# Rotary of the queries in a hybrid trunk: the product with the sines moved ahead of the exchange

## The chip, the cores and the metric

The kernel runs on one core of one Trainium2 chip. A core has five engines, each with its own instruction queue that is executed in order: TensorE (PE; its weight loads are listed as PEld), VectorE (DVE), ScalarE (ACT), GpSimd (POOL) and SyncE (SP), which here only issues DMAs. TensorE writes its results into eight PSUM banks of 128 x 512 fp32 values; DVE and ACT read them there, and everything else lives in SBUF. The metric is the device time of one execution in microseconds (us); the time of a kernel is the median of its runs.

## The reference, cut to what matters

A trunk of two layers over 1024 tokens of width 1024. The even layer has a sparse attention; its 8 attention heads and 8 indexer heads, each of 64 channels, get rotary positions:

```python
def apply_rope(x, cos, sin):
    x1, x2 = jnp.split(x, 2, axis=-1)
    return jnp.concatenate([x1 * cos - x2 * sin, x1 * sin + x2 * cos], axis=-1)
...
    q = apply_rope(q.reshape(B, L, A_HEADS, A_HEAD_DIM), cos[:, None], sin[:, None])
    k = apply_rope(c_kv @ w_uk, cos, sin)
    qi = apply_rope(qi.reshape(B, L, IDX_HEADS, IDX_DIM), cos_i[:, None], sin_i[:, None])
    ki = apply_rope(ki, cos_i, sin_i)
```

The indexer's scores (rectified products of qi and ki, weighted and summed over the heads) choose 256 keys per query, over which q attends. Beside the attention the layer has a pooling mixer over four groups of channels; then come an output projection and an MLP. The odd layer is a gated delta rule and an MLP. All of it is fp32.

## The kernel before, in words

**Layout.** Activations are kept transposed: channels on the 128 partitions, 512 tokens (half of the sequence) on the free axis. The two halves are called s = 0 and s = 1. A matrix product of fp32 precision is made of three (`mm3`, lines 245 to 247): every operand is held as a high part (a rounded copy by ACT, line 165) and a low part (the remainder, a subtraction, line 169, by POOL or DVE). Weights come in chunks by SP (line 200, into `raw`), are copied by ACT and get their remainder from POOL, into the rings `w` and `wm`.

**Even layer.** `even_steps` walks over a list of projections: the latent and the indexer's key first, then four pairs of indexer heads ("qi"), four groups of the pooling mixer ("u"), and four pairs of attention heads ("q"). For each it makes the projection, eight groups of three matmuls into one PSUM bank of the tag "g" (there are two of these), and starts a generator that picks the bank up; then it makes one step of every earlier generator (`step_late`). So what stands behind a `yield` is issued one projection later or more. The pooling group reads its bank with DVE (line 573).

**Rotary of a query pair.** One bank holds two heads, 64 partitions each. For the exchange of the two halves of a head, partitions are exchanged in blocks of 32: partition p gets what lies at p ^ 32. `swapped` (line 502) copies the bank to SBUF with ACT (tile "at") and exchanges the blocks of that copy by four DMAs on SP (line 508), 64 KB each, into a second "at". A step later `query_stacks` (line 350) calls `rotate` (line 334): POOL multiplies the copy by the cosines (line 339, into "temps"), DVE the exchanged parts by the sines (line 340, into "temps") and adds the two (line 341). The table of the sines carries the sign already: -1 on the first 32 partitions of each head, +1 on the others. Then ACT copies the high parts of the two heads, and POOL (s = 0) or DVE (s = 1) makes the remainders (lines 359 and 360). Keys are rotated by the same `rotate` from two banks, the second of which TensorE has filled with the exchanged product, all on DVE.

**Buffers.** `Ring` hands out rotating buffers. "temps" (`self.T`) has five, used by the rotary, the pooling mixer, the sums of squares and the normalized inputs of the MLP (line 327). "at" (`self.A`) has four, used by the rotary, the latent, the indexer's key and the transposed probabilities of the attention (lines 746 to 756). The sines and cosines of one half of the sequence lie in one "rope" buffer, which the other half's overwrite (line 462).

**Order.** The generators set the order in which instructions are issued to a planner, which has its own estimates of durations and puts each engine's instructions into a queue by priority and by when it thinks that their inputs and buffers are ready. The selection of keys (`topk`, lines 671 to 686), a long chain of small DVE and ACT operations, is interleaved with the projections, and for s = 1 the scores (lines 371, 542 to 547) and the attention of s = 0 (`attend`). The last four query projections (s = 1) run beside the normalization for an early part of the MLP, whose matmuls fill the rest of the stage. On the chip the queues are then executed in this fixed order.

Of the kernel before, what the change touches and what calls it, by code (L numbers as in the profile page):

```python
# [18 lines left out]
OP = mybir.AluOpType  # L19
# [105 lines left out]
class Trunk:  # L125
# [205 lines left out]
        return x  # L331


    def rotate(self, p, ps2, s, p_in_psum=False):

        nc = self.nc
        cos, sin = self.ropes[s][:, 0:512], self.ropes[s][:, 512:1024]
        t1, r = self.T.get(), self.T.get()
        (nc.vector if p_in_psum else nc.gpsimd).tensor_tensor(t1, p, cos, op=OP.mult)
        nc.vector.tensor_tensor(r, ps2, sin, op=OP.mult)  # L340
        nc.vector.tensor_tensor(r, r, t1, op=OP.add)
        return r
# [7 lines left out]
    def query_stacks(self, p, s, ring):  # L350

        nc = self.nc
        r = self.rotate(*p, s)
        q = ring.parts()
        a, b = q[:, 0:512], q[:, 512:1024]
        self.copy(a[0:64], r[0:64])
        self.copy(b[64:128], r[64:128])
        eng = nc.vector if s else nc.gpsimd
        eng.tensor_tensor(a[64:128], r[0:64], a[0:64].bitcast(F32), op=OP.subtract)
        eng.tensor_tensor(b[0:64], r[64:128], b[64:128].bitcast(F32), op=OP.subtract)  # L360
        return q
# [92 lines left out]
    def even_latent(self, s, ps):  # L454

        nc = self.nc
        sq, cf = self.T.get(), self.A.get()
        nc.vector.tensor_tensor(cf, ps, self.rb, op=OP.mult)
        nc.scalar.activation(sq, cf, AF.Square)
        yield  # L460
        rope = self.RO.get()
        nc.sync.dma_start(rope, self.I["rope"][s])
        self.ropes.append(rope)
        y = self.rstd_cols(sq, P)
        yield
        r = self.over_partitions(y)
        nc.vector.scalar_tensor_tensor(cf, cf, self.prm[:, R_KVN:R_KVN + 1], r, op0=OP.mult, op1=OP.mult)
        yield
        p1, p2 = self.bank(), self.bank()
        nc.tensor.matmul(p1, self.wkv[:, 0:128], cf, start=True, stop=True)  # L470
        nc.tensor.matmul(p2, self.wkv[:, 128:256], cf, start=True, stop=True)
        self.kst.append(self.key_stacks(self.rotate(p1, p2, s, True), self.KS))
        pv = self.bank()
        for j in range(4):
            nc.tensor.matmul(pv[:, j * 64:(j + 1) * 64], cf[:, j * P:(j + 1) * P], self.wkv[:, 256:320],
                             start=True, stop=True)
        va = self.VA.get()
        self.copy(va, pv[:, :256])
        self.vau.append(va)

    def even_index_keys(self, s, ps):

        nc = self.nc
        kw = self.A.get()
        nc.vector.tensor_tensor(kw[:72], ps[:72], self.rb[:72], op=OP.mult)
        yield
        p1, p2 = self.bank(), self.bank()
        for ps, w in ((p1, self.ident), (p2, self.c(C_SWAP))):
            for at in (0, 64):
                nc.tensor.matmul(ps[at:at + 64], w[:64, 0:64], kw[:64], start=True, stop=True)  # L490
        self.kis.append(self.key_stacks(self.rotate(p1, p2, s, True), self.KI))
        pw = self.bank()
        for j in range(4):
            nc.tensor.matmul(pw[:, j * 8:(j + 1) * 8], kw[:72, j * P:(j + 1) * P],
                             self.cx[:72, C_WSEL:C_WSEL + 8], start=True, stop=True)
        wi = self.small(32, "wi")
        b4 = lambda t: t.rearrange("p (b h) -> p b h", b=4)
        nc.vector.scalar_tensor_tensor(b4(wi), b4(pw[:, :32]), float(np.float32(8 ** -0.5)) / 8,
                                       self.scales[s][0][:, :, None].to_broadcast([P, 4, 8]), op0=OP.mult, op1=OP.mult)
        self.wis.append(wi)  # L500

    def swapped(self, ps):

        pc = self.A.get()
        self.copy(pc, ps)
        ps2 = self.A.get()
        for at in range(0, P, 32):
            self.nc.sync.dma_start(ps2[at:at + 32], pc[at ^ 32:(at ^ 32) + 32])
        return pc, ps2

    def even_index(self, s, p, ps):

        pc = self.swapped(ps)
        yield
        self.qis.append(self.query_stacks(pc, s, self.Y))
        if s == 0:
            for _ in range(1 + (p < 3)):
                yield
            for _ in self.index_scores(s, p):
                pass  # L520
# [35 lines left out]

    def even_query(self, s, p, ps):

        pc = self.swapped(ps)
        yield  # L560
        self.qs[s].append(self.query_stacks(pc, s, self.Q))

# [668 lines left out]
    def even(self):  # L1231

        nc, I = self.nc, self.I
        take = lambda g, n=1: [next(g, None) for _ in range(n)]
        with ExitStack() as st:
            ep = self.pool("even", stack=st, side="left")
            self.mask = {i: ep.tile([P, (i + 1) * P], BF16, name=f"mask{i}") for i in range(2, KT)}
            self.KS, self.VA = Ring(ep, "keys", 2, 1024), Ring(ep, "values", 2, 256)
            self.Q, self.A = Ring(ep, "q", 4, 1024), Ring(ep, "at", 4, 512)
            self.PB, self.rb = Ring(ep, "probs", 4, 1024), ep.tile([P, 512], F32, name="rb")  # L1240
            self.room("a", self.W, self.WM, self.W, self.WM, self.W)
            self.kst, self.vau, self.kis, self.ropes = [], [], [], []
# [251 lines left out]
```

## Time and profile before

| | us |
|---|---|
| time, median of 3 runs | 2784.98 (2773.43 to 2786.07) |
| the profiled execution's own time | 2783.84 |
| its span, first to last instruction | 2782.1 |
| PE busy | 2653.8 (95%) |
| DVE busy | 1660.1 (60%) |
| POOL busy | 1227.5 (44%) |
| ACT busy | 1185.8 (43%) |

How to read what follows. A row of a group or of the list of instructions names the line of the kernel, the engine, the operation, the tile written, "<-" and the tiles read (buffer numbers left out: "at", "temps", "ps_g" for a bank of tag g), and the shapes. In the list of instructions the first two numbers are the start and the duration in us, and a bracket gives how long the engine stood idle before and what ended it. In a list of groups, busy us and mean ns of one stand behind the bar, then the idle time before. In the list of waits, the numbers are us in total, how many times, and the longest. "SPq" and the like are the sequencers that issue DMAs. A matmul's end is modelled by the profiler.

### The profile page before, as it was taken

What the parts mean: (1) busy time and instruction counts of PE and PEld (TensorE: products, weight loads), DVE (VectorE), ACT (ScalarE), POOL (GpSimd) and SP (SyncE); (2) the same over time, 40 slices, a digit from 0 to 9 for tenths busy, and PEclk for the clock granted to TensorE, in tenths of its full rate; (3) what the DMA queues carried; (4) which work ended last, traced back from release to release, by engine and by line L of the source; (5) the groups of instructions that cost most, each with busy time, mean ns of one, the idle gap of its engine ahead of it and who ended that gap; (6) DMA issues with size and microseconds to landing.
All of it is one profiled execution on the core that took longest, in us unless ns stands there. A gap on an engine that the chain in (4) does not pass through costs nothing. (4 is left out here: it accounts for less than half of the span.)

```text
span 2782.1 us, 44603 instructions
## 1 busy us (share of the span) xinstructions
PE 2653.8 (95%) x16640; PEld 2094.9 (75%) x16640; DVE 1660.1 (60%) x3587; ACT 1185.8 (43%) x2480; POOL 1227.5 (44%) x1062
## 2 busy tenths in 40 slices
PE   8789989999999999999999999999999999899998
PEld 6566768787777787777777767777777777688886
DVE  5788998734435655655565777655556645633334
ACT  4557767334444543433333344433334333433332
POOL 4653354542245444434454444434444434544442
PEclk9999989999999999999999999999999999999999
DMA  5221223331123222222222212122222222333332
GB/s 192 76 75 35 68 81 98 91 91 54 42 76 96 80 84 73 80 77 78 68 88 73 62 47 64 59 65 77 75 71 73 69 69 87 118 98 95 96 98 76
DMA packets 121068, 220.91 MB, mean 79 GB/s; under 512 B 14098, under 2 KB 15250, under 8 KB 120850
## 3 DMA queue, kind: packets, MB, share of 16 engines
q1 hardware_dynamic: 120850, 218.05, 25.4%
q8 instruction: 131, 2.15, 0.3%
q14 instruction: 87, 0.71, 0.1%
HBM read 209.61 MB, written 4.19 MB: 77 GB/s over the span
## 5 line engine op out<-in xcount | busy, mean ns | idle before, releaser
L169 POOL TENSOR_TENSOR wm<-raw,wm 128x512 fp32r<-128x512 f32 x425 | 562.0, 1323 | 853.9 <-ACT wm L165 840.3
L165 ACT ACTIVATE wm<-raw 128x512 fp32r<-128x512 f32 x425 | 267.3, 629 | 606.2 <-PE ps_g L246 270.7
L169 POOL TENSOR_TENSOR w<-raw,w 128x512 fp32r<-128x512 f32 x222 | 296.7, 1337 | 351.3 <-ACT w L165 330.8
L841 DVE TENSOR_TENSOR h<-ps_d,h 128x512 f32<-128x512 f32 x392 | 267.1, 685 | 134.4 <-PE ps_d L247 132.4
L245 PE MATMUL ps_g<-x,w 128*128 128x512 f32 x644 | 259.5, 403 | 12.1 <-ACT w L165 9.1
L827 DVE SCALAR_TENSOR_TENSOR ps_g<-ps_g,temps 128x512 f32<-128x512 f32 x128 | 89.1, 696 | 291.0 <-ACT temps L825 291.0
L246 PE MATMUL ps_g<-x,w 128*128 128x512 f32 x644 | 257.1, 399 | 4.3 <-DVE x L380 4.1
L247 PE MATMUL ps_g<-x,w 128*128 128x512 f32 x644 | 256.6, 398 | 1.0 <-POOL w L169 1.0
L245 PE MATMUL ps_d<-y,wm 128*128 128x512 f32 x596 | 243.7, 409 | 10.3 <-DVE h L841 8.7
L165 ACT ACTIVATE w<-raw 128x512 fp32r<-128x512 f32 x222 | 139.0, 627 | 258.3 <-PE ps_g L246 180.9
L247 PE MATMUL ps_d<-y,wm 128*128 128x512 f32 x596 | 236.5, 397 | 0.3 <-POOL wm L169 0.2
L246 PE MATMUL ps_d<-y,wm 128*128 128x512 f32 x596 | 236.0, 396 | 0.0
L245 PE MATMUL ps_g<-xb,wm 128*128 128x512 f32 x512 | 207.7, 406 | 5.6 <-ACT qkvz L947 5.0
L247 PE MATMUL ps_g<-xb,wm 128*128 128x512 f32 x512 | 206.4, 403 | 5.5 <-POOL wm L169 5.4
L246 PE MATMUL ps_g<-xb,wm 128*128 128x512 f32 x512 | 205.7, 402 | 0.0
L949 DVE SCALAR_TENSOR_TENSOR qkvz<-temps,conv,qkvz 128x512 f32<-128x512 f32 x144 | 130.8, 909 | 97.9 <-ACT qkvz L947 96.8
L245 PEld LDWEIGHTS ps_g<-x,w 128*128 128x128 f32 x644 | 123.2, 191 | 40.6 <-ACT w L165 9.9
L245 PE MATMUL ps_g<-x,wm 128*128 128x512 f32 x352 | 141.5, 402 | 7.7 <-ACT wm L165 2.9
L246 PEld LDWEIGHTS ps_g<-x,w 128*128 128x128 f32 x644 | 123.0, 191 | 33.3 <-DVE x L380 6.6
L245 PEld LDWEIGHTS ps_d<-y,wm 128*128 128x128 f32 x596 | 112.0, 188 | 44.9 <-DVE h L841 16.9
L246 PE MATMUL ps_g<-x,wm 128*128 128x512 f32 x352 | 140.9, 400 | 4.4 <-DVE x L169 4.4
L247 PE MATMUL ps_g<-x,wm 128*128 128x512 f32 x352 | 141.1, 401 | 3.2 <-POOL wm L169 3.2
(445 smaller groups left out, 6089.5 us busy)
## 6 DMA issues: line engine op xcount, KB each, us to landing
raw<-in_w_dram SPq DMA_DIRECT2D x456, 256.0 KB, 2.7
raw<-in_woi_dram SPq DMA_DIRECT2D x128, 256.0 KB, 2.6
raw<-in_w2q_dram SPq DMA_DIRECT2D x56, 256.0 KB, 2.6
raw<-in_wei_dram SPq DMA_DIRECT2D x52, 256.0 KB, 2.7
raw<-in_weo_dram SPq DMA_DIRECT2D x32, 256.0 KB, 2.7
raw<-in_woo_dram SPq DMA_DIRECT2D x32, 256.0 KB, 2.7
h<-in_xt_dram SPq DMA_DIRECT2D x16, 256.0 KB, 3.0
at<-at SPq DMA_DIRECT2D x64, 64.0 KB, 2.0
```

The source lines that it names most:

```text
L165: self.nc.scalar.activation(out, in_, AF.Copy)
L169: eng.tensor_tensor(lo, full, hi.bitcast(F32), op=OP.subtract)
L245: mm(ps, wh, xh, start=start, stop=False)
L246: mm(ps, wh, xl, start=False, stop=False)
L247: mm(ps, wl, xh, start=False, stop=stop)
L827: nc.vector.scalar_tensor_tensor(ps, ps, 0.0, r, op0=OP.max, op1=OP.mult)
L841: nc.vector.tensor_tensor(h, ps, h, op=OP.add)
L949: nc.vector.scalar_tensor_tensor(acc, pin[:, j:j + 512], cw(j), acc, op0=OP.mult, op1=OP.add)
```

## The change

The product with the sines is taken before the exchange, directly out of the PSUM bank by DVE (`pm`), instead of after it from the exchanged copy. Since the table's sign is then that of the partition from which the value comes, the exchanged product is subtracted instead of added. ACT still copies the bank to SBUF, and POOL multiplies that copy in place by the cosines, now right behind the copy and not one step later. The four DMAs exchange the blocks of `pm` into `m`. What is left for the later step is one subtraction in place on DVE. A query so uses three "at" buffers (`pc`, `pm`, `m`), of which `pc` is held until its high and low parts are made, and no "temps"; the ring "at" grows from four buffers to six. `rotate` is left to the keys alone.

```diff
-    def rotate(self, p, ps2, s, p_in_psum=False):
+    def rotate(self, p, ps2, s):
 
         nc = self.nc
         cos, sin = self.ropes[s][:, 0:512], self.ropes[s][:, 512:1024]
         t1, r = self.T.get(), self.T.get()
-        (nc.vector if p_in_psum else nc.gpsimd).tensor_tensor(t1, p, cos, op=OP.mult)
+        nc.vector.tensor_tensor(t1, p, cos, op=OP.mult)
         nc.vector.tensor_tensor(r, ps2, sin, op=OP.mult)
         nc.vector.tensor_tensor(r, r, t1, op=OP.add)
         return r
...
     def query_stacks(self, p, s, ring):
 
         nc = self.nc
-        r = self.rotate(*p, s)
+        r, m = p
+        nc.vector.tensor_tensor(r, r, m, op=OP.subtract)
         q = ring.parts()
...
-    def swapped(self, ps):
-
-        pc = self.A.get()
+    def rotated(self, ps, s):
+        nc = self.nc
+        cos, sin = self.ropes[s][:, 0:512], self.ropes[s][:, 512:1024]
+        pc, pm = self.A.get(), self.A.get()
+        nc.vector.tensor_tensor(pm, ps, sin, op=OP.mult)
         self.copy(pc, ps)
-        ps2 = self.A.get()
+        nc.gpsimd.tensor_tensor(pc, pc, cos, op=OP.mult)
+        m = self.A.get()
         for at in range(0, P, 32):
-            self.nc.sync.dma_start(ps2[at:at + 32], pc[at ^ 32:(at ^ 32) + 32])
-        return pc, ps2
+            nc.sync.dma_start(m[at:at + 32], pm[at ^ 32:(at ^ 32) + 32])
+        return pc, m
...
     def even_index(self, s, p, ps):
 
-        pc = self.swapped(ps)
+        pc = self.rotated(ps, s)
         yield
...
     def even_query(self, s, p, ps):
 
-        pc = self.swapped(ps)
+        pc = self.rotated(ps, s)
         yield
...
-            self.Q, self.A = Ring(ep, "q", 4, 1024), Ring(ep, "at", 4, 512)
+            self.Q, self.A = Ring(ep, "q", 4, 1024), Ring(ep, "at", 6, 512)
```

More of the change, by code (lines that the diff above doesn't have):

```diff
@@ L471, in even_latent @@
         nc.tensor.matmul(p2, self.wkv[:, 128:256], cf, start=True, stop=True)
-        self.kst.append(self.key_stacks(self.rotate(p1, p2, s, True), self.KS))
+        self.kst.append(self.key_stacks(self.rotate(p1, p2, s), self.KS))
         pv = self.bank()
@@ L490, in even_index_keys @@
                 nc.tensor.matmul(ps[at:at + 64], w[:64, 0:64], kw[:64], start=True, stop=True)
-        self.kis.append(self.key_stacks(self.rotate(p1, p2, s, True), self.KI))
+        self.kis.append(self.key_stacks(self.rotate(p1, p2, s), self.KI))
         pw = self.bank()
```

## The prediction

> **What bounds the kernel now.** The page comes first, then the busy time by stage.
>
> ```profile
> span 2782.1 us, 44603 instructions
> PE 2653.8 (95%) x16640; PEld 2094.9 (75%) x16640; DVE 1660.1 (60%) x3587; ACT 1185.8 (43%) x2480; POOL 1227.5 (44%) x1062
> ...
> 28.00:410.00 382.00, 332.61 (x1478) 246.00 (x1477) 314.75 (x750) 232.69 (x483) 184.82 (x140) 0.92 0.25 77
> 28.00:160.00 132.00, 110.19 (x441) 79.96 (x439) 95.25 (x241) 70.09 (x148) 80.66 (x65) 0.91 0.33 103
> 350.00:410.00 60.00, 47.11 (x174) 35.38 (x173) 56.55 (x89) 36.13 (x65) 33.85 (x23) 0.83 0.27 80
> 410.00:800.00 390.00, 384.25 (x2044) 311.64 (x2043) 222.44 (x485) 188.09 (x336) 149.29 (x112) 0.99 0.24 74
> L340 DVE TENSOR_TENSOR temps<-at,rope x16: 677/690/1785, 51.4 to 397.0; 128x512 f32<-128x512 f32 x16
> ```
>
> The last row is the answer on the tile "at" (least, median, most ns; first and last start). The columns of the stages are PE, PEld, DVE, ACT, POOL, clock, DMA share, GB/s. PE works 95% of the span. After 410 us it is the bound (384.25 of 390). The 16 products of the queries with the sines start between 51.4 and 397.0 us, so the rotary lies in the stage from 28 to 410 us, and there PE idles 382 - 332.61 = 49.4 us while DVE is busy 314.75 of 382 (82%), and 56.55 of 60 at the end. So what the change can win or lose is settled in 49.4 us of PE's idle time, 21.8 of it before 160 us and 12.9 after 350. The whole is 1.8% of the time.
>
> Who holds PE up there, and who holds DVE and SP up, by the list of waits from 25 or 30 to 410 us:
>
> ```profile
> PE ps_t L371 <- DVE h L547: 6.2, 3, 3.4
> PE ps_g L247 <- POOL wm L169: 3.2, 3, 2.0
> PE ps_g L245 <- ACT at L165: 1.6, 1, 1.6
> PE ps_g L245 <- DVE at L458: 1.6, 1, 1.6
> DVE temps L340 <- DMA at<-at: 9.1, 2, 7.8
> SPq L508 <- ACT at L165: 10.9, 4, 4.5
> ```
>
> PE's longest wait of all is for DVE's score sums (L547), not for the rotary's own instructions. DVE stood 9.1 us, in two places, before the product with the sines (L340), since the exchanged parts had not landed.
>
> **The change part by part.** The groups from 28 to 410 us, by form:
>
> ```profile
> L341 DVE TENSOR_TENSOR temps<-temps 128x512 f32<-128x512 f32 x20 | 19.8, 992 | 0.4
> L340 DVE TENSOR_TENSOR temps<-at,rope 128x512 f32<-128x512 f32 x16 | 16.7, 1046 | 9.2 <-DMA at<-at 9.1
> L340 DVE TENSOR_TENSOR temps<-ps_t,rope 128x512 f32<-128x512 f32 x4 | 2.8, 690 | 1.2 <-PE ps_t L490 1.0 <-PE ps_t L471 0.2
> L339 POOL TENSOR_TENSOR temps<-at,rope 128x512 f32<-128x512 f32 x16 | 24.3, 1522 | 5.9 <-ACT at L165 2.1 <-DVE x L169 2.0 <-DVE ps_s L685 0.8
> ```
>
> Removed: 16 products with the sines from SBUF, 1046 ns each, 16.7 us of DVE. Added: 16 products from the bank. The keys already do this one, at 690 ns: 11.0 us. DVE's load falls by 5.7 us. The subtraction replaces the addition (L341) operand for operand, both in SBUF: 992 ns as before. ACT's copy out of the bank stays. The four DMAs of a query stay, on the same SP queue; they now wait for DVE's product instead of ACT's copy.
>
> Why the SBUF form is dearer shows here:
>
> ```profile
> 49.88 2.52 POOL L339 TENSOR_TENSOR temps<-at,rope 128x512 f32<-128x512 f32 x2
> 49.90 0.69 DVE L339 TENSOR_TENSOR temps<-ps_t,rope 128x512 f32<-128x512 f32 x1 [3.38 <-PE ps_t L470]
> 51.37 1.58 DVE L340 TENSOR_TENSOR temps<-at,rope 128x512 f32<-128x512 f32 x1
> ```
>
> While POOL worked from 49.88 to 52.40, DVE's product out of a bank took 0.69 us and the one with two SBUF inputs 1.58. I therefore take 690 for all 16, in whatever company; the other end is 1046, a saving of nothing.
>
> [...]
>
> *Where the 5.7 us lie on the path.* Two places can be followed.
>
> ```profile
> 57.50 0.58 ACT L165 ACTIVATE at<-ps_g 128x512 f32<-128x512 f32 x1
> 60.74 2.43 SPq L508 DMA_DIRECT2D at<-at  x4
> 66.48 1.72 DVE L340 TENSOR_TENSOR temps<-at,rope 128x512 f32<-128x512 f32 x1 [7.85 <-DMA at<-at]
> ...
> 383.40 1.78 DVE L340 TENSOR_TENSOR temps<-at,rope 128x512 f32<-128x512 f32 x1
> 386.81 1.76 DVE L341 TENSOR_TENSOR temps<-temps 128x512 f32<-128x512 f32 x1
> 388.60 1.28 ACT L165 ACTIVATE q<-temps 64x512 fp32r<-64x512 f32 x2 [3.91 <-DVE temps L341]
> 389.90 0.63 ACT L165 ACTIVATE wm<-raw 128x512 fp32r<-128x512 f32 x1
> 390.59 0.57 PE L245 MATMUL ps_g<-x,wm 128*128 128x512 f32 x1 [2.92 <-ACT wm L165]
> ```
>
> At 57.50 a query leaves its bank; SP issues its DMAs only at 60.74, DVE waits until 66.48, and the score work behind it starts late, which PE feels at L547. The new product fits before 60.74, where DVE was idle (from 66.48 - 7.85 = 58.63), so the DMAs are no earlier and DVE still waits; but behind the landing one operation stands instead of two. That is 1.72 us less; I count -1.5, between 0 and the 6.2 that PE lost to L547.
>
> At 383.40 the same operation precedes the addition, ACT's copies and, queued behind them on ACT, a weight for which PE waits 2.92 us. Without it all move up: -1.8, between 0 and -2.9.
>
> The other queries free 0.36 us each on a DVE that is 82% busy while PE idles 13%: some 4 us; I count -1.0, between 0 and -4.
>
> *The buffers.* A query held two "temps" buffers of five (T) and two "at" of four (A); now it holds none of T and three of six of A. From 365 to 387 us the early MLP's normalized inputs pass through T:
>
> ```profile
> 375.70 0.51 PE L245 MATMUL ps_g<-x,wm 128*128 128x512 f32 x1 [2.35 <-ACT x L165]
> 379.79 0.79 PE L246 MATMUL ps_g<-x,wm 128*128 128x512 f32 x1 [3.58 <-DVE x L169]
> ...
> 381.20 1.73 POOL L339 TENSOR_TENSOR temps<-at,rope 128x512 f32<-128x512 f32 x1 [2.01 <-DVE x L169]
> ```
>
> POOL's product of a query waited for a buffer of T that the normalization gave back (L169), so both compete for it. PE lost 2.35 + 3.58 = 5.9 us to these inputs. Freed buffers are worth 0 to -5.9; I take -1.5, near the lower end, as DVE itself is full there. Against it, the products of two queries move from behind this normalization into it: 2 x 0.69 = +1.4.
>
> *The hold of the bank.* There are two banks for projections. A bank was free after ACT's copy; now it needs ACT's copy and DVE's product.
>
> ```profile
> 77.26 0.39 PE L247 MATMUL ps_g<-x,w 128*128 128x512 f32 x1
> 82.08 0.68 DVE L573 TENSOR_TENSOR temps<-ps_g,rb 128x512 f32<-128x512 f32 x1
> ...
> 353.39 0.39 PE L247 MATMUL ps_g<-x,w 128*128 128x512 f32 x1
> 359.78 0.39 PE L247 MATMUL ps_g<-x,w 128*128 128x512 f32 x1
> 363.86 0.58 ACT L165 ACTIVATE at<-ps_g 128x512 f32<-128x512 f32 x1
> ```
>
> The pooling projections show what a pick-up by DVE is like: the latest comes 82.08 - 77.65 = 4.4 us after the last matmul, while ACT's copy of a query came 363.86 - 360.17 = 3.7 us after its own. The last matmuls of two queries lie 6.4 us apart, which is the time until a bank is wanted again; both lags fit into it. In the list of waits, banks freed by ACT cost PE 1.6 us once, and banks freed by DVE (L458) 1.6 once. So the 16 x 0.69 = 11.0 us of longer hold are hidden behind the other bank's project; without that cover they cost 11.0. I take one exposed product, +0.7, where PE already waits for ACT's copy.
>
> *POOL's product*, the same instruction now in place, is issued right behind the copy instead of a step later, ahead of weight remainders (L169). At 1522 ns it could push three weights for which PE waits: 0 to +4.6. I take 0, because POOL idles 52% of the time from 28 to 410 us.
>
> **Sum:** -1.5 - 1.8 - 1.0 - 1.5 + 1.4 + 0.7 = -3.7 us, against the profiled execution's own 2783.84 us (span 2782.1 plus 1.7 around it): 2780.1, say **2780**. The profiled time is 1.1 us under the median of the runs, 2784.98; their spread, 2773.43 to 2786.07, is larger than the change. All gains at their ends (-6.2 - 2.9 - 4 - 5.9, without the +2.1) give 2765; all losses at theirs (+11.0 + 4.6 + 1.4, no gain) give 2801; a mixture of half of each keeps the likeliest case within 2770 to 2792.
>
> **The rivals.**
> - *The buffers and the shorter chain open the stage.* The instruction order is planned anew around five free T buffers. If half of PE's idle time before 160 us (21.8) and after 350 us (12.9) goes, that is 17 us: 2766. For it: DVE's 9.1 us of waiting and POOL's wait for a buffer. Against it: DVE is 94% busy after 350 us whatever the buffers. 24%.
> - *The bank hangs on DVE (slower).* DVE executes in order. If a product stands behind a waiting instruction, the lag is the 4.4 us of the pooling plus a wait of up to 7.85: 12.3 us, that is 5.9 over the 6.4 that the other bank covers. Behind it stand SP's four DMAs, and behind them the weights' loads. It decides from a lag over 6.4 us; three such hits cost 17.7 us: 2801. For it: DVE's load. Against it: eight pooling projections live with DVE's pick-up without a wait of PE. 13%.
> - *POOL's early product delays the weights:* +4.6 on top of a lost gain, 2788. For it: PE waits 3.2 us for POOL's remainders. Against it: POOL's idle half. 15%.
> - *Nothing of it reaches PE:* DVE has less to do and PE waits as before, 2784. 13%.
>
> **How the numbers follow.** The forecast itself has 35%, the rivals 24, 13, 15 and 13. A measurement tells about 0.5%, 13.9 us: under 2771 is faster, over 2799 slower. The first rival and little of the forecast's edge are faster: 26%; the second, mostly, is slower: 12%; the rest, 62%, is no difference. The range 2764 to 2799 takes in the first rival and the bounds, and leaves out the end of the second.
>
> **What would show it.** Right: the bank's product at 0.69 us with few above; L340's SBUF form gone; DVE's total down by about 6 us; a wait of the subtraction for the DMA still near 60 us; PE's idle time from 28 to 410 us at 43 to 49 us. Wrong: PE's first matmul of a project waiting for the bank's product by more than 2 us in total, SP's exchange waiting on DVE far over 10.9 us, or PE's idle time after 410 us moved by over 5 us, which nothing here accounts for.

## The result, and the profile after

The changed kernel takes **2758.91 us** (median of 7 runs, 2752.86 to 2768.38), the kernel before 2780.19 (median of 7, 2773.43 to 2786.07): a ratio of **0.9931**, 95% interval 0.9911 to 0.9950. That is 19 us less (14 to 25), or 0.7%, clear of the noise, and 2758.91 is below the predicted range of 2764 to 2799. Beside the gain this has a second part: the kernel before came out 4.8 us under the median of 2784.98 that stood ahead of the prediction. The profiled execution of the changed kernel took 2764.82 us, with a span of 2763.0.

The page of the changed kernel and its busy time by stage (columns as in the prediction: PE, PEld, DVE, ACT, POOL, clock, DMA share, GB/s):

```profile
span 2763.0 us, 44585 instructions
PE 2647.6 (96%) x16640; PEld 2095.2 (76%) x16640; DVE 1645.7 (60%) x3587; ACT 1184.6 (43%) x2480; POOL 1224.6 (44%) x1062
...
28.00:410.00 382.00, 343.39 (x1567) 259.96 (x1566) 318.43 (x789) 247.57 (x510) 190.80 (x147) 0.95 0.26 82
28.00:160.00 132.00, 113.93 (x472) 85.34 (x470) 96.98 (x264) 73.62 (x155) 84.27 (x68) 0.91 0.34 109
160.00:270.00 110.00, 100.42 (x521) 73.05 (x520) 92.90 (x252) 72.91 (x167) 37.29 (x30) 0.97 0.16 49
350.00:410.00 60.00, 52.21 (x208) 40.96 (x207) 56.09 (x98) 43.31 (x79) 36.54 (x25) 0.91 0.29 85
410.00:800.00 390.00, 386.52 (x2060) 313.47 (x2059) 208.35 (x455) 181.62 (x322) 154.20 (x115) 1.00 0.25 75
```

PE's idle time from 28 to 410 us fell from 49.4 to 382 - 343.39 = 38.6 us, under the 43 to 49 that the prediction gave as a sign of being right. That is 10.8 us of the gain. A second part is in the clock column: 0.92 became 0.95. Busy time multiplied by the granted clock goes here with the matmuls done: 332.61 x 0.92 = 306 us for 1478 of them before, 343.39 x 0.95 = 326 for 1567 after, 0.207 and 0.208 us each. That is 20 us of work at full clock more by the same moment, so about 9 of these come from the clock (each product is good to 2 us, the clock being given to two digits). The split is that of two single profiles. Another profile of the program before (the run with the background's lead at 49, below) has the same idle time, 382 - 332.33 = 49.7 us, with a clock of 0.94, which leaves 3 us for the clock; and "temps" back, a variant as fast as the changed kernel, has 382 - 335.73 = 46.3 us of idle time with a clock of 0.96.

That PE is ahead at 410 us is seen directly in the first and last start of two lines, first of the kernel before, then of the changed one. The upper line of each is the addition after the even layer's output projection, the lower one the early MLP's:

```profile
L816 DVE TENSOR_TENSOR h<-ps_g,h x16: 684/691/693, 306.7 to 844.0; 128x512 f32<-128x512 f32 x16
L841 DVE TENSOR_TENSOR h<-ps_t,h x128: 667/692/694, 428.4 to 2766.7; 128x512 f32<-128x512 f32 x128
```

```profile
L824 DVE TENSOR_TENSOR h<-ps_g,h x16: 684/691/692, 294.7 to 819.9; 128x512 f32<-128x512 f32 x16
L849 DVE TENSOR_TENSOR h<-ps_t,h x128: 667/691/694, 406.6 to 2747.1; 128x512 f32<-128x512 f32 x128
```

The first addition of the output projection comes 12.0 us earlier, the first of the early MLP 21.8 us, the last of all 19.6 us. So the gain is made before 410 us, in the stage that the prediction named, and nearly half of it between 300 and 410 us (these differences are good to some 6 us, as a second profile of the program before shows below).

The groups of the rotary in the changed kernel, from 28 to 410 us, and its waits from 25 to 410 us:

```profile
L354 DVE TENSOR_TENSOR at<-at 128x512 f32<-128x512 f32 x16 | 16.6, 1040 | 4.8 <-DMA at<-at 3.5 <-POOL at L513 1.2
L511 DVE TENSOR_TENSOR at<-ps_g,rope 128x512 f32<-128x512 f32 x15 | 10.3, 685 | 4.7 <-PE ps_g L247 4.6
L513 POOL TENSOR_TENSOR at<-at,rope 128x512 f32<-128x512 f32 x16 | 21.9, 1366 | 8.9 <-DVE ps_s L694 3.4 <-ACT at L165 3.3 <-DVE ps_s L693 2.0
...
PE ps_t L372 <- DVE h L555: 6.2, 2, 4.2
PE ps_g L245 <- ACT at L165: 5.8, 2, 3.5
PE ps_g L247 <- POOL wm L169: 2.3, 3, 1.0
DVE at L354 <- DMA at<-at: 3.5, 1, 3.5
```

The product out of the bank (L511; the 16th has the first bank, of another tag) costs 685 ns (690 were predicted), and the subtraction (L354) 1040 instead of the addition's 992. DVE's wait for the exchange fell from 9.1 us to 3.5. PE's waits for the score sums (L555) did not change. PE's waits for a bank that ACT has to copy rose from 1.6 us to 5.8: that speaks against the change. SP's exchange waits on DVE for 12.3 us in its own list of waits, after 10.9 on ACT before, so the sign of "far over 10.9 us" did not come.

One query shows what was gained. In the kernel before, it is the one that left its bank at 107.39 us (lists of instructions of ACT, DVE and PE):

```profile
107.39 0.58 ACT L165 ACTIVATE at<-ps_g 128x512 f32<-128x512 f32 x1
...
121.53 0.68 DVE L340 TENSOR_TENSOR temps<-at,rope 128x512 f32<-128x512 f32 x1
122.31 0.69 DVE L341 TENSOR_TENSOR temps<-temps 128x512 f32<-128x512 f32 x1
...
124.16 1.26 ACT L165 ACTIVATE q<-temps 64x512 fp32r<-64x512 f32 x2
126.17 0.58 ACT L165 ACTIVATE at<-ps_g 128x512 f32<-128x512 f32 x1
...
126.80 0.50 PE L245 MATMUL ps_g<-x,w 128*128 128x512 f32 x1 [1.64 <-ACT at L165]
```

The same query in the changed kernel:

```profile
102.75 0.68 DVE L511 TENSOR_TENSOR at<-ps_g,rope 128x512 f32<-128x512 f32 x1
109.74 1.51 DVE L354 TENSOR_TENSOR at<-at 128x512 f32<-128x512 f32 x1
...
111.28 1.28 ACT L165 ACTIVATE q<-at 64x512 fp32r<-64x512 f32 x2 [1.04 <-DVE at L354]
120.25 0.60 ACT L165 ACTIVATE at<-ps_g 128x512 f32<-128x512 f32 x1
```

Before, 15.6 us pass from the start of the pick-up to the end of the addition (122.31 + 0.69 - 107.39); after, 8.5 us to the end of the subtraction. ACT's copies of the finished query (124.16) therefore fell close ahead of its copy of the next query's bank (126.17), for which PE stood 1.64 us; after the change they end 7.7 us before that copy (111.28 + 1.28 against 120.25), and the matmul behind it does not wait.

### The profile page after: what moved, and what is told of

It is laid out like the page before. It is cut to its first block, busy times and chain, and to the rows that moved or that the text cites. A ratio compares the mean times of both kernels' runs of the same rounds, so it can differ in the third digit from the quotient of the medians.

```text
span 2763.0 us, 44585 instructions
## 1 busy us (share of the span) xinstructions
PE 2647.6 (96%) x16640; PEld 2095.2 (76%) x16640; DVE 1645.7 (60%) x3587; ACT 1184.6 (43%) x2480; POOL 1224.6 (44%) x1062
## 5 line engine op out<-in xcount | busy, mean ns | idle before, releaser
L245 PE MATMUL ps_g<-x,w 128*128 128x512 f32 x644 | 258.3, 401 | 11.2 <-ACT w L165 9.4
L245 PEld LDWEIGHTS ps_g<-x,w 128*128 128x128 f32 x644 | 122.6, 191 | 39.1 <-ACT w L165 10.1
L245 PE MATMUL ps_g<-x,wm 128*128 128x512 f32 x352 | 142.3, 404 | 10.3 <-ACT at L165 5.8
L246 PEld LDWEIGHTS ps_g<-x,w 128*128 128x128 f32 x644 | 122.5, 190 | 32.0 <-DVE x L381 5.7
L247 PE MATMUL ps_g<-x,wm 128*128 128x512 f32 x352 | 141.7, 403 | 2.3 <-POOL wm L169 2.3
L247 PEld LDWEIGHTS ps_g<-x,w 128*128 128x128 f32 x644 | 122.5, 190 | 27.6 <-POOL w L169 1.4
```

Of the source, the lines that this page charges most:

```text
L245: mm(ps, wh, xh, start=start, stop=False)
L246: mm(ps, wh, xl, start=False, stop=False)
L247: mm(ps, wl, xh, start=False, stop=stop)
```

## The experiments

Each was timed in 5 rounds beside the kernel before; its median there was 2776.87 to 2780. The ratio is to that. The last column is where the profile has the first addition of the early MLP, which comes after everything that the change touches.

| kernel | ratio, 95% interval | median us | first early-MLP addition, us |
|---|---|---|---|
| before | 1 | 2780.19 | 428.4 |
| changed | 0.9931 (0.9911 to 0.9950) | 2758.91 | 406.6 |
| before, background's lead 49 (the same program) | 0.9999 (0.9989 to 1.0010) | 2777.56 | 422.2 |
| before, background's lead 20 | 0.9994 (0.9982 to 1.0005) | 2776.05 | 422.0 |
| before, ring of six | 1.0008 (0.9998 to 1.0018) | 2779.43 | 423.2 |
| before, ring of six and no "temps" | 0.9988 (0.9974 to 1.0003) | 2774.30 | 423.8 |
| changed, product from the SBUF copy | 0.9963 (0.9949 to 0.9976) | 2766.44 | 413.6 |
| changed, copy ahead of the product | 0.9958 (0.9942 to 0.9974) | 2766.51 | 409.6 |
| changed, "temps" back | 0.9936 (0.9922 to 0.9950) | 2760.38 | 407.8 |
| changed, POOL's product a step later | 0.9923 (0.9905 to 0.9940) | 2757.59 | 406.8 |
| changed, both products on DVE | 0.9939 (0.9923 to 0.9955) | 2762.98 | 402.9 |
| changed, pick-up planned ahead | 0.9938 (0.9923 to 0.9953) | 2760.56 | 410.1 |
| changed, one operation more behind the landing | 0.9974 (0.9962 to 0.9987) | 2770.44 | 416.6 |
| changed, one operation more ahead of the exchange | 0.9942 (0.9927 to 0.9957) | 2762.36 | 406.1 |
| changed, ring of four | 0.9949 (0.9931 to 0.9967) | 2764.82 | 415.7 |
| changed, subtraction on POOL | 0.9993 (0.9980 to 1.0006) | 2775.64 | 420.3 |

**The buffers alone.** The ring of the kernel before, and nothing else:

```diff
-            self.Q, self.A = Ring(ep, "q", 4, 1024), Ring(ep, "at", 4, 512)
+            self.Q, self.A = Ring(ep, "q", 4, 1024), Ring(ep, "at", 6, 512)
```

> The kernel before with the ring "at" of six buffers instead of four, and nothing else. The change as a whole took 21.3 us off the median, half of which stands in the profile as less idle time of PE from 28 to 410 us (49.4 to 38.6) and half as a higher granted clock there (0.92 to 0.95). Theory of the buffers: the two "at" buffers are one of two reliefs, worth 3 to 8 us, in the query projections from 350 us on. Theory of the bank product: 0 within 3 us. Theory of the plan (any edit gives another order, and the order gives or takes up to 10 us by chance): anything from -10 to +10 us.

1.0008: six buffers by themselves are worth nothing (at most 0.02%, by the interval).

**The buffers, and "temps" freed.** With the same ring, the queries' `rotate` works in place in the two "at" buffers, after the exchange as before:

```diff
-        t1, r = self.T.get(), self.T.get()
+        t1, r = (self.T.get(), self.T.get()) if p_in_psum else (p, ps2)
```

> The kernel before with six "at" buffers and the rotary's three operations in place in them (copy times cosines, exchanged copy times sines, sum), so that a query uses no "temps"; products, sources and order of issue are as before. Theory of the buffers: most of the 21 us comes, 12 to 21, and the inputs of the early MLP no longer hold PE up for 5.9 us. Theory of the bank product: nothing beyond the ring of six alone. Theory of the plan: -10 to +10 us.

0.9988, an interval that includes 1. All buffers that the change frees are free here, and at most 0.26% comes of it.

**"temps" back into the changed kernel,** the other direction: the difference goes to a buffer of "temps".

```diff
-        r, m = p
-        nc.vector.tensor_tensor(r, r, m, op=OP.subtract)
+        t1, m = p
+        r = self.T.get()
+        nc.vector.tensor_tensor(r, t1, m, op=OP.subtract)
```

> The changed kernel with the difference written into a buffer of "temps", held until the parts of the query are made, as the sum was before; the rest as changed. Six "at" buffers alone gave 1.0008, in-place operations without "temps" in the old order 0.9988. Theory of the buffers as a part (about 0.1%): 0.994. Theory that freed "temps" matter only together with the new order: 0.996 or more.

0.9936, as the changed kernel. From both sides the freed buffers are not distinct from zero; an effect of the forecast size, 1.5 us or 0.05%, is too small for these runs.

**The place of the product without the bank.** The product is taken ahead of the exchange, but behind ACT's copy and from it:

```diff
-        nc.vector.tensor_tensor(pm, ps, sin, op=OP.mult)
         self.copy(pc, ps)
+        nc.vector.tensor_tensor(pm, pc, sin, op=OP.mult)
```

> The changed kernel, but the product with the sines is taken from ACT's copy in SBUF instead of the bank (copy first, then the product, still ahead of the exchange). The bank is then held by ACT alone and the product has two SBUF inputs. Theory of the bank product: DVE's product rises from 685 towards 1046 ns (5.8 us more on DVE) and at least 6 of the 21 us are lost. Theory of the buffers: the same time as the changed kernel within 4 us. If what costs in the changed kernel is ACT's copy standing behind DVE's product (PE waits 5.8 us for such copies at 364 and 378 us), it is faster than the changed kernel by up to 8 us.

0.9963. The 16 products are as dear as ever, on average 1111 ns, so none of the predicted 5.7 us is saved, and yet about half of the gain is there. This half comes from the place of the product, not from its price.

**The bank's product behind the copy.** Only the order of the two readers of the bank is changed:

```diff
-        nc.vector.tensor_tensor(pm, ps, sin, op=OP.mult)
         self.copy(pc, ps)
+        nc.vector.tensor_tensor(pm, ps, sin, op=OP.mult)
```

> The changed kernel with ACT's copy of the bank issued ahead of DVE's product instead of behind it; sources, buffers and operations are the same. In the changed kernel's trace the copy always starts after the product has ended (ACT stood 6.9 and 2.5 us for it at 356 to 363 and 374 to 377 us). If the two reads of a bank are kept in the order of issue, DVE now waits for ACT instead. Theory of the bank product (the gain is DVE's 5.7 us and the earlier exchange): 0.993 of the kernel before or up to 0.2% lower, as PE's 5.8 us of waiting for copies go. Theory of the plan (another order alone moves the time): 0.993 to 1.000 or better, by chance.

0.9958, no better than the product from SBUF, although the product is down to 683 ns. Its instructions at 360 to 371 us show where part of it went:

```profile
361.97 0.57 ACT L165 ACTIVATE at<-ps_g 128x512 f32<-128x512 f32 x1
369.54 0.68 DVE L512 TENSOR_TENSOR at<-ps_g,rope 128x512 f32<-128x512 f32 x1
370.37 0.77 PE L245 MATMUL ps_g<-x,wm 128*128 128x512 f32 x1 [12.23 <-DVE at L512]
```

ACT had copied the bank by 362.54, DVE's product of it stood behind the early MLP's normalization until 369.54, and PE stood 12.23 us. This is the mechanism of the rival on the slower side: one hit instead of the three that it named, and twice its price of 5.9 us for each.

**POOL's product a step later,** at the head of `query_stacks` as before the change:

```diff
-        nc.gpsimd.tensor_tensor(pc, pc, cos, op=OP.mult)
...
         r, m = p
+        nc.gpsimd.tensor_tensor(r, r, self.ropes[s][:, 0:512], op=OP.mult)
```

> The changed kernel with POOL's product with the cosines issued a step later again, right before the subtraction. Theory of the shorter chain (behind the landed exchange one operation stands on DVE instead of two, and POOL's product was early enough in either place): 0.993 as the changed kernel. Theory of the early product (the subtraction no longer waits for POOL, whose queue is in order): 0.996 to 0.998, that is 8 to 14 us lost.

0.9923, an interval that overlaps the changed kernel's: POOL's early product neither helps nor delays weights by an amount that shows.

**Both products on DVE,** without ACT's copy and POOL's product:

```diff
-        self.copy(pc, ps)
-        nc.gpsimd.tensor_tensor(pc, pc, cos, op=OP.mult)
+        nc.vector.tensor_tensor(pc, ps, cos, op=OP.mult)
```

> The changed kernel with both products taken out of the bank by DVE; ACT's copy and POOL's product fall away. DVE gets 16 x 0.69 = 11.0 us more, ACT 9.3 us and POOL 22 us less, and the bank is held for two products one behind the other, 1.4 us. If DVE is what holds PE up in the stage, 2 to 10 us slower than the changed kernel (0.994 to 0.997 of the kernel before); if the wait of the copy behind the product and POOL's queue cost more than DVE's time, up to 6 us faster (0.991).

0.9939. DVE has 16 operations more (680 ns each, 10.9 us), all ahead of the exchange, ACT and POOL have 16 less each, and the time is that of the changed kernel.

**Order alone.** Two changes of the plan with the old rotary. The first, the background's lead at 49 places instead of 50, has every engine's instructions in the very order of the kernel before; it shows only how far two runs of one program differ.

```diff
-        self.background, self.masked, self.pace, self.solo, self.hurry = [], {0, 1}, 3, False, 50
+        self.background, self.masked, self.pace, self.solo, self.hurry = [], {0, 1}, 3, False, 49
```

> The kernel before with one number of the planner's priorities changed from 50 to 49 (how far the selection of keys is pulled ahead); no operation, buffer or source is changed. It measures what another order alone is worth. Theory of the plan: a difference of 4 to 10 us either way. Theories of the buffers and of the bank product: within 3 us of the kernel before.

0.9999, and its profile has a span of 2775.9 us where that of the kernel before has 2782.1. So two profiles of one program differ by 6 us, and the 21.8 us by which the early MLP begins earlier are uncertain by as much (its own time there: 422.2 instead of 428.4). The second changes the order in fact, with both places that set the lead:

```diff
-        self.background, self.masked, self.pace, self.solo, self.hurry = [], {0, 1}, 3, False, 50
+        self.background, self.masked, self.pace, self.solo, self.hurry = [], {0, 1}, 3, False, 20
...
-                self.hurry = 50
+                self.hurry = 20
```

> The kernel before with the background work (the search for the largest scores) planned 20 places ahead instead of 50, so that the order of some instructions changes on every engine (95 lines of difference on TensorE, 201 on VectorE) and the rotary does not. Plan theory (a new order by itself moves the time as far as the change did): off by 0.3 to 0.7% to either side. Theory of the rotary's own chain: 0.998 to 1.002.

0.9994: this new order moves nothing by itself. It is a much smaller reshuffle than that of the change. A larger one is on hand: the ring of six without "temps" has the old rotary as well. Compared line by line with the kernel before, by operation, tile and shape, the order of TensorE's instructions in the profiles differs in 26 lines with the lead of 20, in 156 without "temps" and in 124 in the changed kernel; VectorE's in 80, 306 and 226. So an order as far from the old one as that of the change came to 0.9988 (0.9974 to 1.0003). That makes the plan an unlikely cause of 0.7%, and does not exclude that this one order was a lucky one.

**One operation more, at two places.** This pair has the same load and differs in the place. Behind the landing:

```diff
         r, m = p
+        nc.vector.tensor_scalar(m, m, 1.0, None, op0=OP.mult)
         nc.vector.tensor_tensor(r, r, m, op=OP.subtract)
```

> The changed kernel with one more VectorE operation for each of the 16 queries, a multiplication of the landed exchange by 1.0, between the landing and the subtraction. Chain theory (what counts is how little stands behind the landing of the exchange, as in the product and the addition that became one subtraction): about half of the gain goes, ratio 0.996 to 0.998. Load theory (16 operations of some 0.4 to 0.7 us cost VectorE 6 to 11 us at any place): 0.995 to 0.996, the same as the kernel with the operation ahead of the exchange. If neither place nor load matters: 0.992 to 0.994.

And ahead of the exchange:

```diff
         self.copy(pc, ps)
+        nc.vector.tensor_scalar(pm, pm, 1.0, None, op0=OP.mult)
```

> The changed kernel with the same extra multiplication by 1.0 on the product itself, behind the copy in program order and ahead of the four transfers: the exchange leaves later by it, the bank comes free as before, and one subtraction stands behind the landing. Theory of the early exchange (the 0.3% between product first and copy first is the earlier departure of the exchange): 0.995 to 0.997, as with copy first. Chain theory (behind the landing alone): 0.992 to 0.994. Load theory: 0.995 to 0.996, equal to the kernel with the operation behind the landing.

The groups from 28 to 410 us, first with the operation behind the landing, then with it ahead of the exchange:

```profile
L355 DVE TENSOR_TENSOR at<-at 128x512 f32<-128x512 f32 x16 | 14.2, 889 | 0.4
L354 DVE TENSOR_SCALAR at<-at 128x512 f32<-128x512 f32 x16 | 13.8, 865 | 5.1 <-DMA at<-at 5.1
```

```profile
L354 DVE TENSOR_TENSOR at<-at 128x512 f32<-128x512 f32 x16 | 16.0, 1002 | 4.2 <-DMA at<-at 3.9 <-issue 0.3
L513 DVE TENSOR_SCALAR at<-at 128x512 f32<-128x512 f32 x16 | 12.1, 756 | 0.1
```

Against the changed kernel's 16.6 us of subtractions, the first adds 13.8 + 14.2 - 16.6 = 11.4 us to DVE, the second 12.1 + 16.0 - 16.6 = 11.5. The first comes to 0.9974, the second to 0.9942, and the intervals do not overlap. **Behind the landing 11.4 us cost 0.43% or 12 us, about one for one; ahead of the exchange the same cost 0.11% or 3 us,** which is within the uncertainty of nothing (each difference is good to about 0.23%, 6 us). The exchange also leaves later in the second, by the operation's 756 ns at least, so an early departure of that size is not what the change wins.

**The subtraction on POOL.** DVE is relieved of all that stands behind the landing:

```diff
-        nc.vector.tensor_tensor(r, r, m, op=OP.subtract)
+        nc.gpsimd.tensor_tensor(r, r, m, op=OP.subtract)
```

> The changed kernel with the subtraction behind the landed exchange on GpSimd instead of VectorE. VectorE loses 16 operations of 1.04 us (16.6 us) and GpSimd gets 16 of about 1.4 us. Load theory (VectorE's seconds count at any place): 0.988 to 0.990. Chain theory (what counts is the time from the landing to the finished query): the operation is some 0.4 us longer and stands behind weight remainders on GpSimd, each with a wait for ScalarE in front, so the query is later, not earlier: 0.994 to 0.998.

```profile
L354 POOL TENSOR_TENSOR at<-at 128x512 f32<-128x512 f32 x16 | 22.5, 1404 | 3.1 <-DMA at<-at 3.0
...
28.00:410.00 382.00, 332.61 (x1518) 251.71 (x1517) 307.41 (x749) 240.42 (x496) 206.35 (x160) 0.94 0.25 79
```

The group and the stage of this kernel: DVE is busy 307.41 us instead of 318.43, the operation behind the landing takes 1404 ns instead of 1040, and the whole gain is gone, 0.9993. PE idles 49.4 us again, as before the change. DVE's load is not the limit. The expectation's reason for the loss does not hold, though: in the lists of instructions, from the first DMA of a query's exchange, on SP, to the end of the operation behind the landing pass 7.4 us on average over the 16 queries, less than the 8.7 of the changed kernel (14.9 before the change, to the end of the addition). And to the end of the query's low parts it is 16.6 us, as with "temps" back (16.7), where the gain is all there (changed kernel 16.0, before 19.4). What the change loses here stays open; the longer operation and the weight remainders that now stand behind it on POOL are candidates.

**The bank's pick-up ahead.** The changed kernel's two waits for banks (below) should go when product and copy are planned ahead of the normalization:

```diff
-        nc.vector.tensor_tensor(pm, ps, sin, op=OP.mult)
-        self.copy(pc, ps)
+        with self.ahead_by(200):
+            nc.vector.tensor_tensor(pm, ps, sin, op=OP.mult)
+            self.copy(pc, ps)
```

> The changed kernel, in which the bank's product and the copy of every query are planned 200 places earlier than their place in the program, so that they need not stand behind the normalization of the early MLP. Bank theory (the changed kernel still loses 3.48 + 2.29 us at 364 and 377 us because the product stands behind the normalization on VectorE, and the copy behind the product): both waits shrink under 1 us, the ratio to the kernel before goes from 0.993 to 0.990 or 0.991. Load theory (VectorE's seconds count, not their place): 0.993 as the changed kernel. Plan theory (every new order of the instructions moves the time by some tenths of a per cent, whatever the reason of the edit): anywhere from 0.990 to 0.998.

Its waits of PE from 300 to 415 us:

```profile
PE ps_g L246 <- DVE x L169: 3.6, 1, 3.6
PE ps_g L245 <- ACT at L165: 2.7, 1, 2.7
PE ps_g L245 <- DVE y L169: 2.0, 1, 2.0
PE ps_g L247 <- POOL wm L169: 1.9, 1, 1.9
```

The waits for the bank fell from 5.8 us to 2.7, but PE now waits 3.6 us for the normalization that the pick-up overtook; the ratio is 0.9938, no gain. The bank theory failed: the wait moved from the bank to the normalization, both of which are DVE's work at this place.

**The ring of four in the changed kernel:**

```diff
-            self.Q, self.A = Ring(ep, "q", 4, 1024), Ring(ep, "at", 6, 512)
+            self.Q, self.A = Ring(ep, "q", 4, 1024), Ring(ep, "at", 4, 512)
```

> The changed kernel with the ring of the tile at left at four buffers, as before; a query holds three of them. Theory that the ring is only room (with the ring of six alone nothing moved): the third buffer of a query is taken from the next one, whose product then waits for a subtraction, so part of the gain goes: 0.994 to 0.997. Theory that the ring of six carries nothing: 0.992 to 0.994, as the changed kernel.

0.9949 lies in the first theory's range, and its interval overlaps the changed kernel's. Whether the two further buffers carry a little of the gain stays open; most of it is there without them.

No variant is clearly better than the change: the best, POOL's product a step later (0.9923), has an interval that contains the changed kernel's ratio.

## Why the prediction was wrong, point by point

The stage and the direction were right; the size was not: -3.7 us were forecast, 19 were measured. **The step that failed is the price of the other queries,** "free 0.36 us each on a DVE that is 82% busy [...] I count -1.0, between 0 and -4". It took the change as a saving of DVE time and kept the shorter chain for two places alone. The runs show another currency. One more operation in the query's second step, behind the landed exchange, costs about its full time (12 us for 11.4), and in its first step little (3 us for 11.5), each good to 6 us. With the prices of the pair of experiments, the 16.7 us of L340 that leave the second step are worth some 17 us, and the 10.3 us of L511 in the first step cost some 3 (10.3 x 3 / 11.5). This estimate gives -14, at the edge of the measured 14 to 25. It also fits the product from SBUF: -17 and 17.8 x 3 / 11.5 = +5 make -12, and 0.9963 is -10. It was made after the runs, and the price ahead of the exchange is uncertain by twice its size.

Why the second step is dear is read off one place and not proven: for the query at 107 us ACT's copies stand behind the addition, and behind these on ACT stands the next bank's copy, for which PE waits. That the sum is early is not enough: with the subtraction on POOL it comes 7.4 us after the first DMA of the exchange and nothing is won, with "temps" back it comes after 11.9 us and all of the gain is there, and with one operation more behind the landing it comes after 11.2 us and over half of the gain is lost. So the price of the place is measured, for operations on DVE, and its mechanism is open.

In the prediction's own arithmetic one bound is off: half of all gains, 9.5 us, gives 2774 as the lower end of its likeliest case, not 2770. Nothing above rests on it.

The other terms:

- **The query at 57 to 66 us, -1.5.** DVE's wait there went, from 7.85 us to none (the subtraction starts at 62.63 us; the 3.5 us in the list belong to the next query), but PE's waits for the score sums, through which it should have been felt, stayed at 6.2 us. At the one place that was followed, the query at 107 us, the gain came through ACT's queue.
- **383 to 390 us, -1.8.** The direction was right: the wait of 2.92 us is gone. By the profile before it was worth more than itself, for the reason below.
- **The freed buffers, -1.5.** Not distinct from nothing in the runs on them, 0.26% or 7 us at the most. They are not what gives the 19 us.
- **Two products in the normalization and the hold of the bank, +1.4 and +0.7.** The mechanism was right, and its sum of 2.1 us was too small: PE waited 5.8 us in two places (rows of the changed kernel, list of instructions):

```profile
362.70 0.69 DVE L511 TENSOR_TENSOR at<-ps_g,rope 128x512 f32<-128x512 f32 x1
363.43 0.60 ACT L165 ACTIVATE at<-ps_g 128x512 f32<-128x512 f32 x1 [6.92 <-DVE at L511]
364.08 0.79 PE L245 MATMUL ps_g<-x,wm 128*128 128x512 f32 x1 [3.48 <-ACT at L165]
...
377.04 0.60 ACT L165 ACTIVATE at<-ps_g 128x512 f32<-128x512 f32 x1 [2.50 <-DVE at L511]
377.69 0.50 PE L245 MATMUL ps_g<-x,wm 128*128 128x512 f32 x1 [2.29 <-ACT at L165]
```

  The prediction added the product to the copy; that ACT, free for 6.92 us, waits for DVE's product before it copies the same bank, was not seen. The sign of "PE's first matmul waiting over 2 us", given as proof of a wrong forecast, came true, and the kernel is faster all the same: what this sign measures is outweighed.
- **POOL's product, 0.** Right.
- **The price of the bank's product, 690 ns.** Right (685). With the product behind the copy, SBUF or bank as its source made no difference to the time (0.9963 and 0.9958), though one wait of 12.23 us may hide what the bank saves. DVE's busy total fell by 14.4 us instead of 6; where the rest comes from stays open.
- **PE's idle time after 410 us.** Within 5 us, as said: of the 12.9 us by which all idle time fell (128.3 to 115.4 us), 10.8 lie before 410.

**Three gaps of PE cost more than their length** (2.92, 3.48 and 3.58 us). This can bear on every term, and the prediction quoted its row (0.83 from 350 to 410 us) without using it. The kernel before, behind its gap of 3.58 us at 379.79, in its list of instructions, and then by stretches:

```profile
380.81 0.63 PE L245 MATMUL ps_g<-x,wm 128*128 128x512 f32 x1
...
383.37 0.63 PE L245 MATMUL ps_g<-x,wm 128*128 128x512 f32 x1
...
384.38 0.39 PE L245 MATMUL ps_g<-x,wm 128*128 128x512 f32 x1
...
385.07 0.39 PE L245 MATMUL ps_g<-x,wm 128*128 128x512 f32 x1
```

```profile
380.00:385.00 5.00, 5.00 (x14) 3.96 (x15) 5.00 (x5) 3.51 (x6) 3.80 (x3) 0.60 0.02 5
390.00:400.00 10.00, 7.02 (x15) 4.11 (x16) 9.82 (x15) 5.08 (x9) 4.31 (x3) 0.54 0.18 56
```

The seven matmuls from 380.81 to 383.37 (two of every three left out above) start 0.43 us apart, the four from 384.38 to 385.07 0.23. The granted clock from 380.4 to 384 us is 0.50. From 390 to 400 us, behind the gap of 2.92 us, the granted clock is 0.54 and 15 matmuls run. The same stretch of time in the changed kernel, without a gap, and its own stretch with the gap of 3.48 us at 364.08:

```profile
390.00:400.00 10.00, 10.00 (x45) 8.15 (x44) 8.78 (x21) 8.76 (x18) 4.76 (x5) 1.00 0.39 114
363.00:370.00 7.00, 4.41 (x10) 3.01 (x11) 6.93 (x13) 4.34 (x8) 4.64 (x3) 0.54 0.17 40
```

45 matmuls in place of 15 from 390 to 400 us; but the changed kernel pays behind its own gap too, with a clock of 0.54 and matmuls 0.43 us apart up to 373.8 us. Behind its gap of 2.29 us at 377.69 the matmuls start 0.23 us apart.

So the rate is about halved behind these gaps, 0.43 against 0.23 us from start to start, and for how long differs: some 3.5 us behind the first, from 380.4 to 384, and 14 us behind the second, of 2.92 us, to 404.6, with gaps of 0.64 and 1.61 us in it. Nor is the price fixed for one program: in the other profile of the kernel before (lead 49) the same gap of 2.92 us, there at 386.18, is followed by the half rate for only 5.7 us. That gaps give the gain from the clock (3 to 9 us by 410 us, by the profile that is taken as before) is a reading of the rows; no run changed the gaps alone.

**The rivals.** The first, an opened stage at 2766 us, came nearest; of its two causes the buffers are out (at most 0.26%), and the shorter second step is what is left. The rival that the bank hangs on DVE exists as a mechanism (5.8 us here, 12.23 with the copy first) and is outweighed. POOL's delay of weights does not appear (PE's waits for its remainders, 3.2 us before, are 2.3).

**What stays open.** The changed kernel and its near relatives with the product first (0.9923 to 0.9942) are some 0.2% better than the two with it behind the copy (0.9958, 0.9963). The 12.23 us of the one are located; whether the other's loss, PE waits of 2.54 and 3.87 us for the normalization at 369.73 and 381.06 us, follows from the order or from the plan was not settled.

## What to carry to other kernels

When an operation is moved across a transfer, do not price it only by what it costs its engine, but by where it stands: here an operation behind the landing cost about its full time (12 us for 11.4), and the same one ahead of the transfer little or nothing (3 us for 11.5, good to 6). To learn the price of a place, put one idle operation there and the same one elsewhere: the pair costs two runs and separates the load from the place. It does not tell why the place is dear, and the price need not hold when the operation goes to another engine. And look at the matmuls behind a gap of PE of some three microseconds: here they ran at half rate for 14 us behind one of 2.92 us, and for 5.7 us behind the same gap in another execution of the program.

## What was not expected of the hardware

- ACT's copy and DVE's product of the same bank overlap for none of the 16 queries: in the changed kernel a copy starts 0.04 us after the product's end even where ACT was idle for 6.92 us before. With the order turned round, DVE waits for the copy: 3.4 of its 3.6 us of idle time before the products end with it. Whether the order of the two is imposed by the program's semaphores or by the bank was not tested.
- Between 360 and 410 us, matmuls behind gaps of 2.92 to 3.58 us ran at half rate, for 3.5 to 14 us (granted clock down to 0.54 over 10 us), those behind one of 2.29 us did not, and the clock stayed at 1.00 from 380 to 410 us in the changed kernel, where no such gap is left. Behind the same gap of 2.92 us, two executions of one program had the half rate for 14 and for 5.7 us.
- One program gave profiles 6.2 us apart in span (2782.1 and 2775.9), with clocks of 0.92 and 0.94 from 28 to 410 us. A difference of that size between single profiles of two kernels says nothing.
